# Seven block products in place of eight for two of eight pairs of inner tiles, in ten gate and up groups of a feed-forward stage

## The chip, the cores and the metric

The kernel runs on one core of a Trainium2 chip. The metric is the device time of one execution in microseconds; lower is better. The core has five engines that run side by side and meet at semaphores: TensorE (PE in the profile, with PEld for its weight loads) does matmuls, VectorE (DVE) and ScalarE (ACT) do elementwise work, GpSimd (POOL) and SyncE (SP) issue transfers here. Each engine takes its instructions in the order in which the program lists them for it.

## The reference, cut to what matters

One encoder block: four parallel mixers, cross attention, and a gated feed-forward part, each added to the residual, and a last norm. The change lies in the feed-forward part, for 256 rows, `D_MODEL` 2048 and `D_FF` 5632, all in float32:

```python
def swiglu(h, w_gate_up, w_down):
    gate, up = jnp.split(h @ w_gate_up, 2, axis=-1)
    return (jax.nn.silu(gate) * up) @ w_down

x = x + swiglu(rms_norm(x, norm_g[l, 2]), w_gate_up[l], w_down[l])
```

## The kernel before

**Float32 products in three matmuls.** The weights and activations are float32. Each operand is kept as a high part, rounded to the matmul's operand type, and a low part, the difference. A product of a 128x128 block of activations and a 128x512 block of weights is three matmuls into one PSUM bank: high by high, high by low, low by high (`part_rows`, L349, L350, L351). The activations are the stationary operand, the weights the moving one. An activation tile has 512 columns: 256 rows high, 256 rows low.

**The weight stream.** All weights arrive in one stream of slabs of 16 blocks of 128x128, that is 128x2048, 1 MB each, in the order in which they are used (`Stream`, L61 to L121). SP loads a slab into one of three `raw` buffers (L81). `_half` (L75) prepares half a slab, a piece of 1024 columns, at a time: ScalarE copies it to the high part `wh` (L102), VectorE subtracts to get the low part `wl` (L103). `take` (L107) hands out four blocks at a time; at the start of each piece it lets `_half` run so far ahead that two further pieces are prepared or in preparation, three if an extra pool `st.extra` is open. There are three pairs of `wh` and `wl` buffers, and a fourth with the extra pool, so the copy of a piece waits until TensorE is done with the piece that had its buffer.

**The background.** Work that isn't on the main path is written as generators. `Background.poll` (L160), called after each product, steps a generator if its due time has come and if VectorE owes little by the program's own accounts; `drain` (L165) steps one to its end at once. The program order that results is fixed when the kernel is built.

**The gate and up stage** (`gate_up`, L874) has 11 groups of 512 columns of the gate and the same 512 of the up half. A group goes through 16 inner tiles of 128 for the gate (16 x 2 row halves = 32 products, into two banks), then the same for up; together 64 products and 8 slabs. `gate` (L879) takes SiLU from the gate's banks on ScalarE (L882). `up` (L884) multiplies on VectorE (L206), transposes (L390) and stores to the tensor `hidden` in HBM through POOL. The first group takes the inner tiles in parts, since the last of them arrive late; groups 1 to 10 are alike (L928 to L930). The background task `fetch` (L891) loads tiles of `hidden` back (L397) and splits them into the feature tiles `f` (L210, L202): 28 of 44 beside the groups (L927), the last 16 in the next stage (L932), since they lie in `self.h3`, the activation tiles that the groups still read.

**The down stage** (`down`, L934) goes through the 44 feature tiles four times, two products a step, and forces `fetch` on if a feature tile isn't ready three steps ahead.

Of the kernel before, what the change touches and what calls it, by code (L numbers as in the profile page):

```python
# [34 lines left out]
CUTS = {0: [0, 256, 512, 1024, 2048]}  # L35
# [25 lines left out]
class Stream:  # L61


    def __init__(self, tc, pools, W, bg):
        self.tc, self.nc, self.W, self.bg = tc, tc.nc, W, bg
        self.rawp, self.wp = pools
        self.order = []
        self.n = 0
        self.after = []
        self.halves = []  # L70
        self.raw = None
        self.extra = None
        self.places = []

    def _half(self):  # L75

        nc, n = self.nc, 8 * len(self.halves)
        if n % 16 == 0:
            self.raw = self.rawp.tile([P, 2048], F32, name="raw", tag="raw")
            for a, b in zip(CUTS[n], CUTS[n][1:]) if n in CUTS else [(0, 1024), (1024, 2048)] if self.after else [(0, 2048)]:  # L80
                (nc.scalar if (n, a) == (0, 0) else nc.sync).dma_start(self.raw[:, a:b], self.W[n // 16][:, a:b])  # L81
                if self.after:
                    self.after.pop(0)()
# [12 lines left out]
        pool = self.extra if self.extra and len(self.halves) % 4 == 3 else self.wp  # L96
        wh, wl = (pool.tile([P, 1088], F32R, name=t, tag=t) for t in ("wh", "wl"))
        at = 48 if any(a <= n < b for a, b in ROWS) else 8
        wh, wl = wh[:, at:at + 1024], wl[:, at:at + 1024]
        edges = [0, 256, 512, 1024] if n == 0 else [0, 512, 1024] if n == 8 else [0, 1024]  # L100
        for a, b in zip(edges, edges[1:]):
            nc.scalar.copy(wh[:, a:b], r[:, a:b])  # L102
            nc.vector.tensor_tensor(out=wl[:, a:b], in0=r[:, a:b], in1=wh[:, a:b].bitcast(F32), op=ALU.subtract)  # L103
        self.bg.dve(1024)
        self.halves.append((wh, wl))

    def take(self, w, k, c, nb=1):  # L107
        if self.n % 8 == 0:
            ahead = self.n // 8 + 1 + min(3 if self.extra else 2, self.n // 16)
            while len(self.halves) < min(ahead, NBLK // 8):  # L110
                self._half()
        half, o = self.halves[self.n // 8], (self.n % 8) * P
        if self.n >= NBLK - HELD:
            (wh, wl), o = half[o // 512], 0
        else:
            wh, wl = half
        self.order += [(w, k, c + i * P) for i in range(nb)]
        self.n += nb
        if self.n % 8 == 0:
            self.halves[self.n // 8 - 1] = None  # L120
        return wh[:, o:o + nb * P], wl[:, o:o + nb * P]  # L121


class Background:
# [17 lines left out]
    def first(self, g):  # L142

        self.q.sort(key=lambda e: e[0] is not g)
# [29 lines left out]
class Block:  # L174
# [25 lines left out]
    def tt(self, out, a, b, op):  # L200
        self.bg.dve(math.prod(out.shape[1:]))
        self.nc.vector.tensor_tensor(out=out, in0=a, in1=b, op=op)  # L202
# [139 lines left out]
    def part_rows(self, p, r, slot, wh, wl, start, stop, narrow=False):  # L342

        if narrow:
            for c in (slice(0, R), slice(R, 512)):
                self.part_rows(p[:, c], r, slot, wh[:, c], wl[:, c], start and c.start == 0, stop)
            return
        hi, lo = slot[:, r * P:(r + 1) * P], slot[:, R + r * P:R + (r + 1) * P]
        self.nc.tensor.matmul(p, hi, wh, start=start, stop=False)  # L349
        self.nc.tensor.matmul(p, hi, wl, start=False, stop=False)  # L350
        self.nc.tensor.matmul(p, lo, wh, start=False, stop=stop)  # L351
        self.bg.pe(0.68 * wh.shape[1] / 512)

    def gemm_rows(self, w, cols, slots, done=None, parts=None, before=None, out=None):

# [506 lines left out]
    def mlp(self):  # L862
        tc, nc, act = self.tc, self.nc, self.act
        with tc.tile_pool(name="fp", bufs=1) as fp:
            self.gap(fp, 192)
            f = act[4:12] + [fp.tile([P, 512], F32R, name=f"f{i}") for i in range(20)] + self.h3
            with tc.tile_pool(name="gp", bufs=2) as gp:
                self.gate_up(gp, f)
# [5 lines left out]
    def gate_up(self, gp, f):  # L874

        nc = self.nc
        box, g, stored = {}, {}, []

        def gate(ps):  # L879
            for r in range(2):  # L880
                g[r] = gp.tile([P, 512], F32, name=f"g{r}", tag=f"g{r}")
                nc.scalar.activation(g[r], ps[r], AF.Silu, scale=box["col"][:, r:r + 1])  # L882

        def up(j, ps):  # L884
            for r in range(2):
                h, u = (gp.tile([P, 512], F32, name=n, tag=n) for n in ("h", "u"))
                self.stt(h, ps[r], box["col"][:, r:r + 1], g[r], ALU.mult, ALU.mult)
                self.store_turned(self.ff, 4 * j, r, u, h)
            stored.append(self.bg.now)

        def fetch(k0, k1, ahead, pause, wait=0):  # L891
# [32 lines left out]
        self.bg.drain(col)  # L924
        gate(ps[0])
# [722 lines left out]
```

## Time and profile before

| | |
|---|---|
| time, three runs | 1462.64, 1463.66 and 1462.53 us, median 1462.64 |
| profiled execution | span 1461.5 us from first to last instruction; its own time is not listed apart from the runs |
| granted TensorE clock | mean 0.998 |
| moved by DMA | 320.15 MB, mean 219 GB/s |
| loads of `raw` by SP | 246 of 1024 KB, 11 of 512 KB |

How to read it: all times are microseconds unless marked ns. Part 1 of the page has busy time and share of each engine, part 2 cuts the span into 40 slices with busy tenths, part 4 follows the chain of work that ended last back from the end, part 5 lists groups of instructions with line, engine, operation, output, inputs and count, then busy time, the mean of one in ns, and the engine's idle time just before them with what ended it. In the order of single instructions the columns are start, duration, engine, line, operation, output, inputs and count, and in brackets the idle time before. Neighbouring instructions of one engine can overlap, so a duration can be longer than the distance between two starts.

### The profile page before, as it was taken

Reading aid. Unit: us, or ns where it says so; the run is one execution under the profiler, and the core shown is the slowest. Engines: PE = TensorE matmul, PEld = TensorE weight load, DVE = VectorE, ACT = ScalarE, POOL = GpSimd, SP = SyncE. Lnnn points to the kernel's source line nnn. Section 1 sums busy time; section 2 is a strip of 40 time slices with the busy share of each in tenths; the row PEclk is TensorE's granted clock in tenths of the full one; section 3 lists DMA queues with packets and bytes.
Section 4 is the critical chain, followed back from the end, with each engine's and each line's share of the span. In section 5 each row is a group of like instructions: output and inputs, shape, how many; then the busy total and the mean of one; then the engine's idle time right before and its main releaser. Section 6 shows DMA issues by size and latency. Waiting matters only on the chain.

```text
span 1461.5 us, 17996 instructions
## 1 busy us (share of the span) xinstructions
PE 1452.1 (99%) x6724; PEld 1206.9 (83%) x6724; DVE 920.9 (63%) x1319; ACT 735.2 (50%) x1048; POOL 207.8 (14%) x276
## 2 busy tenths in 40 slices
PE   9999999999999999999999999999999999999997
PEld 7888888888888888888888888888888888888886
DVE  6668868777887676676665555455555456444445
ACT  7566655447555465565554444444444445434344
POOL 0000100012302333530411110011110011000000
PEclk9999999999999999999999999999999999999999
DMA  9877555456757788864867666666766666555554
GB/s 353 295 284 248 200 200 173 145 202 211 229 185 243 243 251 260 253 209 150 257 227 228 213 218 211 213 215 228 229 206 212 216 217 219 198 193 186 197 201 144
DMA packets 60071, 320.15 MB, mean 219 GB/s; under 512 B 9517, under 2 KB 11214, under 8 KB 28368
## 3 DMA queue, kind: packets, MB, share of 16 engines
q1 hardware_dynamic: 46208, 281.11, 56.0%
q0 software_dynamic: 13344, 37.24, 9.8%
q8 instruction: 52, 0.85, 0.2%
q10 hardware_dynamic: 432, 0.66, 0.1%
q14 instruction: 35, 0.29, 0.1%
HBM read 298.52 MB, written 20.45 MB: 218 GB/s over the span
## 4 chain that ended last, share of the span: by engine, by line
PE 99%; DMA 0%; ACT 0%; SPq 0%; DVE 0%; issue 0%
PE pg L349 29%; PE pg L351 29%; PE pg L350 29%; PE pg L300 4%; PE pg L301 2%; PE pm L1101 1%; PE pm L855 1%; PE pm L351 1%; PE pm L349 1%; PE pm L350 1%; PE pm L826 1%; DMA raw<-in_W 0%; PE pm L1510 0%; PE pm L827 0%; PE pm L1275 0%; PE pm L1062 0%
## 5 line engine op out<-in xcount | busy, mean ns | idle before, releaser
L103 DVE TENSOR_TENSOR wl<-raw,wh 128x1024 fp32r<-128x1024 f32 (+1 forms) x503 | 611.5, 1216 | 477.5 <-ACT wh L102 476.5
L102 ACT CAST wh<-raw 128x1024 fp32r<-128x1024 f32 (+1 forms) x503 | 524.0, 1043 | 597.8 <-PE pg L351 527.5
L349 PE MATMUL pg<-wh,act 128*128 128x512 f32 (+1 forms) x1666 | 650.2, 390 | 0.1
L350 PE MATMUL pg<-wl,act 128*128 128x512 f32 (+1 forms) x1666 | 648.4, 389 | 0.5 <-DVE wl L103 0.5
L351 PE MATMUL pg<-wh,act 128*128 128x512 f32 (+1 forms) x1666 | 648.6, 389 | 0.0
L349 PEld LDWEIGHTS pg<-wh,act 128*128 128x128 f32 x1666 | 313.0, 188 | 66.4 <-issue 1.5
L351 PEld LDWEIGHTS pg<-wh,act 128*128 128x128 f32 x1666 | 312.9, 188 | 65.6 <-DVE act L202 0.2
L350 PEld LDWEIGHTS pg<-wl,act 128*128 128x128 f32 x1666 | 313.0, 188 | 65.1 <-DVE wl L103 1.1
L300 PE MATMUL pg<-act,wh 128*128 128x512 f32 x256 | 90.5, 395 | 0.0
L301 PE MATMUL pg<-act,wl 128*128 128x256 f32 x256 | 71.8, 280 | 0.0
L392 POOL DMA_DIRECT2D hidden<-u x22 | 16.7, 763 | 386.5 <-DVE u L390 386.5
L300 PEld LDWEIGHTS pg<-act,wh 128*128 128x128 f32 x256 | 48.1, 188 | 10.5
L351 PE MATMUL pg<-wh,f 128*128 128x512 f32 x140 | 54.5, 389 | 0.0
L349 PE MATMUL pg<-wh,f 128*128 128x512 f32 x140 | 54.5, 389 | 0.0
L350 PE MATMUL pg<-wl,f 128*128 128x512 f32 x140 | 54.5, 389 | 0.0
L301 PEld LDWEIGHTS pg<-act,wl 128*128 128x128 f32 x256 | 48.2, 188 | 0.2
L397 POOL DMA_DIRECT2D tmp<-hidden x44 | 38.9, 890 | 39.5 <-ACT wh L102 24.3
L392 POOL DMA_DIRECT2D features<-tmp x32 | 22.8, 717 | 95.9 <-DVE tmp L390 95.9
L351 PEld LDWEIGHTS pg<-wh,f 128*128 128x128 f32 x140 | 26.3, 188 | 5.5
L350 PEld LDWEIGHTS pg<-wl,f 128*128 128x128 f32 x140 | 26.3, 188 | 5.4
L349 PEld LDWEIGHTS pg<-wh,f 128*128 128x128 f32 x140 | 26.3, 188 | 5.3
L397 POOL DMA_DIRECT2D ar<-features x24 | 21.1, 888 | 20.7 <-DMA features<-tmp 13.0
(314 smaller groups left out, 1046.0 us busy)
## 6 DMA issues: line engine op xcount, KB each, us to landing
raw<-in_W SPq DMA_DIRECT2D x246, 1024.0 KB, 5.0
raw<-in_W SPq DMA_DIRECT2D x11, 512.0 KB, 7.0
hidden<-u POOLq DMA_DIRECT2D x22, 256.0 KB, 3.5
tmp<-hidden POOLq DMA_DIRECT2D x44, 128.0 KB, 5.1
features<-tmp POOLq DMA_DIRECT2D x32, 128.0 KB, 2.7
ar<-features POOLq DMA_DIRECT2D x24, 128.0 KB, 6.5
k<-in_mem SPq DMA_DIRECT2D x8, 256.0 KB, 7.6
keys<-k POOLq DMA_DIRECT2D x8, 256.0 KB, 7.4
```

The source lines that it names most:

```text
L102: nc.scalar.copy(wh[:, a:b], r[:, a:b])
L103: nc.vector.tensor_tensor(out=wl[:, a:b], in0=r[:, a:b], in1=wh[:, a:b].bitcast(F32), op=ALU.subtract)
L300: self.nc.tensor.matmul(p[:, :], wh, slot[:, :], start=start, stop=False)
L301: self.nc.tensor.matmul(p[:, 0:R], wl, slot[:, 0:R], start=False, stop=stop)
L349: self.nc.tensor.matmul(p, hi, wh, start=start, stop=False)
L350: self.nc.tensor.matmul(p, hi, wl, start=False, stop=False)
L351: self.nc.tensor.matmul(p, lo, wh, start=False, stop=stop)
L392: self.nc.gpsimd.dma_start(to[r], u.rearrange("p (k c) -> p k c", c=P))
L397: self.nc.gpsimd.dma_start(t.rearrange("p (g t) -> p g t", t=32), src)
L826: nc.tensor.matmul(p[:, :], q[d][:, r * P:(r + 1) * P], kt[d][:, :], start=d == 0, stop=False)
L855: nc.tensor.matmul(p[:, 0:R], v[m][:, s], pt[m][:, c:c + R], start=m == 0 and v is vh and c == 0, stop=m == 1 and v is vl)
L1101: self.b.nc.tensor.matmul(p, a, b, start=start and n == 0, stop=stop and n == 2)
```

## The change

In groups 1 to 10, the inner tiles 0 and 1, and 2 and 3, are taken as two pairs. For a pair, the activations are a 2x2 block matrix (two row halves by two inner tiles), and the weights are one too (two inner tiles by gate and up). Their block product is done in seven products in place of eight. The other twelve tiles are taken as before.

The plan of a group is `GROUP = "NNSNNSNN"`, one letter per slab. N is a slab as before. S is the slab of a pair: `_sums` makes four pieces of it, of 1024, 512, 1024 and 1024 columns; ahead of the third it sums blocks of `raw` in place, four additions of 512 columns on VectorE. The pieces serve 2, 1, 2 and 2 products, each against one 128x128 block of activations. Three of a pair's seven use activations as they are, four use combinations that `combine` makes in new tiles `z`, once, between group 0 and group 1.

```diff
+GATE_UP = 1920 // 16 + 8
+GROUP = "NNSNNSNN"
+
+PAIRED = {GATE_UP + 8 * j + i for j in range(10) for i, x in enumerate(GROUP) if x == "S"}
...
+    def _sums(self):
+
+        nc, r, ph = self.nc, self.raw, self.phase
+        o, m = ((0, 1024), (1024, 512), (0, 1024), (1024, 1024))[ph]
+        wh, wl = self._buffers(self.made, m)
+        if ph == 2:
+            s = [r[:, i * 512:i * 512 + 512] for i in range(4)]
+            for out, a, b in ((1, 1, 3), (3, 0, 3), (0, 0, 1), (2, 0, 2)):
+                nc.vector.tensor_tensor(out=s[out], in0=s[a], in1=s[b], op=ALU.add)
+            self.bg.dve(2048, 4)
+        src = r[:, o:o + m]
+        nc.scalar.copy(wh, src)
+        nc.vector.tensor_tensor(out=wl, in0=src, in1=wh.bitcast(F32), op=ALU.subtract)
+        self.bg.dve(src.shape[1])
+        self.halves.append((wh, wl))
+        self.phase = (ph + 1) % 4
+        if ph == 3:
+            self.made += 16
+
+    def _fill(self):
+
+        ahead = self.at + 1 + min(3 if self.extra else 2, self.n // 16)
+        while len(self.halves) < ahead and self.made < NBLK:
+            self._half()
...
+    def combine(self, z, a, b):
+
+        tt, t, u, v, w = self.tt, *(self.tmp() for _ in range(4))
+        for x, y in ((t, a), (u, b)):
+            tt(x, y[:, 0:R].bitcast(F32), y[:, R:512].bitcast(F32), ALU.add)
+        yield SOON
+        tt(v[:, 0:P], t[:, P:R], u[:, P:R], ALU.subtract)
+        tt(w[:, 0:P], t[:, 0:P], t[:, P:R], ALU.subtract)
+        tt(v[:, P:R], v[:, 0:P], t[:, 0:P], ALU.subtract)
+        tt(w[:, P:R], u[:, 0:P], v[:, P:R], ALU.add)
+        yield SOON
+        for i, x in enumerate((v, w)):
+            self.split2(z[:, i * R:i * R + R], z[:, 512 + i * R:512 + i * R + R], x)
```

`paired_rows` takes gate and up together. Its products go to eight PSUM banks: four of the pool `pg` for gate and up by row half (`a0`, `a1`, `b0`, `b1`), and four of the pool `pm` for the products 1, 5, 6 and 7, which several results share. Both S slabs add into the same banks. The shared ones are combined behind the second S (`mixed`), then the gate is finished (`gated`); up is finished at the group's end (`upped`).

```diff
+        for kind in plan:
+            if kind == "S":
...
+                pairs = iter((("1", a[0]), ("b0", x4), ("a0", a[1]), ("6", s2), ("7", s3), ("a1", a[2]), ("5", x1)))
+                for parts in st.take_sums(w, ks, cols):
+                    for wh, wl in parts:
+                        name, (hi, lo) = next(pairs)
+                        put(name, hi, lo, wh, wl)
+                        self.bg.poll()
+                done += 1
+                if done == s:
+                    mixed(*(q[i] for i in "1567"))
...
+            if first and done == s and n >= len(rest):
+                first(q["a0"], q["a1"])
+                first = None
...
+        def mixed(q1, q5, q6, q7):
+
+            g[0], g[1], h[0], h[1] = (gp.tile([P, 512], F32, name=n, tag=n) for n in ("g0", "g1", "h", "h"))
+            nc.scalar.copy(g[0], q1)
+            self.tt(h[0], g[0], q6, ALU.add)
+            self.tt(g[1], h[0], q7, ALU.add)
+            self.tt(h[0], q5, h[0], ALU.subtract)
+            self.tt(h[1], q5, g[1], ALU.subtract)
+
+        def gated(*ps):
+
+            for r in range(2):
+                self.tt(g[r], g[r], ps[r], ALU.add)
+                nc.scalar.activation(g[r], g[r], AF.Silu, scale=box["col"][:, r:r + 1])
+
+        def upped(j, ps):
+
+            for r in range(2):
+                self.tt(h[r], h[r], ps[r], ALU.add)
+            up(j, h, h)
```

The rest in the stage: the extra pool (`wy`, a fourth pair of weight buffers) is open throughout it, the combinations are drained between groups 0 and 1, and `z` is used again for four feature tiles, so that 24 feature tiles are fetched beside the groups and 20 in the down stage.

```diff
+            with tc.tile_pool(name="wy", bufs=1) as self.st.extra, tc.tile_pool(name="gp", bufs=2) as gp:
+                self.gate_up(gp, f, z)
+                self.st.extra = None
...
+        sums = [((2 * i, 2 * i + 1), z[i]) for i in range(GROUP.count("S"))]
+        comb = self.bg.add(combined())
         gate(ps[0])
         up(0, ps[1])
-        early = self.bg.add(fetch(0, FT - 16, 3, 2.0, 15))
+        early = self.bg.add(fetch(0, FT - 20, 3, 2.0, 15))
+        self.bg.drain(comb)
         for j in range(1, DFF // 512):
-            gate(self.gemm_rows("w_gate_up", [j * 512], self.h3)[0])
-            up(j, self.gemm_rows("w_gate_up", [DFF + j * 512], self.h3)[0])
+            upped(j, self.paired_rows("w_gate_up", [j * 512, DFF + j * 512], self.h3, sums, GROUP, mixed, gated))
         self.bg.drain(early)
-        self.bg.add(fetch(FT - 16, FT, 6, SOON))
+        self.bg.add(fetch(FT - 20, FT, 6, SOON))
```

More of the change, by code (lines that the diff above doesn't have):

```diff
@@ L67, in __init__ @@
         self.order = []
-        self.n = 0
+        self.n = self.made = 0
         self.after = []
         self.halves = []
+        self.at = self.phase = 0
         self.raw = None
@@ L73, in __init__, with _buffers, _load @@
         self.places = []
-    def _half(self):
[L77 to L83, printed above, removed]
+    def _buffers(self, n, m):
+        pool = self.extra if self.extra and len(self.halves) % 4 == 3 else self.wp
+        at = 48 if any(a <= n < b for a, b in ROWS) else 8
+        return (pool.tile([P, 1088], F32R, name=t, tag=t)[:, at:at + m] for t in ("wh", "wl"))
+    def _load(self, n):
+        nc = self.nc
+        self.raw = self.rawp.tile([P, 2048], F32, name="raw", tag="raw")
+        for a, b in zip(CUTS[n], CUTS[n][1:]) if n in CUTS else [(0, 1024), (1024, 2048)] if self.after else [(0, 2048)]:
+            (nc.scalar if (n, a) == (0, 0) else nc.sync).dma_start(self.raw[:, a:b], self.W[n // 16][:, a:b])
+            if self.after:
+                self.after.pop(0)()
+    def _half(self):
+        nc, n = self.nc, self.made
+        if n % 16 == 0 and self.phase == 0:
+            self._load(n)
+        if n // 16 in PAIRED:
+            return self._sums()
+        self.made += 8
         o = (n % 16) * P
@@ L95, in _half @@
             return
[L96 to L99, printed above, removed]
+        wh, wl = self._buffers(n, 1024)
         edges = [0, 256, 512, 1024] if n == 0 else [0, 512, 1024] if n == 8 else [0, 1024]
@@ L105, in _half, with _used @@
         self.halves.append((wh, wl))
-    def take(self, w, k, c, nb=1):
[L108 to L112, printed above, removed]
+    def _sums(self):
[19 more added lines that the diff above has]
+            self._half()
+    def _used(self):
+        self.halves[self.at] = None
+        self.at += 1
+    def take(self, w, k, c, nb=1):
+        o = (self.n % 8) * P
+        if o == 0:
+            self._fill()
+        half = self.halves[self.at]
         if self.n >= NBLK - HELD:
@@ L119, in take, with take_sums @@
         if self.n % 8 == 0:
-            self.halves[self.n // 8 - 1] = None
+            self._used()
         return wh[:, o:o + nb * P], wl[:, o:o + nb * P]
+    def take_sums(self, w, ks, cols):
+        assert self.n // 16 in PAIRED and self.n % 16 == 0
+        self.order += [(w, ks[k], cols[c] + i * P) for k, c in ((0, 0), (1, 1), (1, 0), (0, 1)) for i in range(4)]
+        for ph in range(4):
+            self._fill()
+            wh, wl = self.halves[self.at]
+            yield [(wh[:, a:a + 512], wl[:, a:a + 512]) for a in range(0, wh.shape[1], 512)]
+            self._used()
+        self.n += 16
 class Background:
@@ L347, in part_rows, with part @@
             return
-        hi, lo = slot[:, r * P:(r + 1) * P], slot[:, R + r * P:R + (r + 1) * P]
+        self.part(p, slot[:, r * P:(r + 1) * P], slot[:, R + r * P:R + (r + 1) * P], wh, wl, start, stop)
+    def part(self, p, hi, lo, wh, wl, start, stop):
         self.nc.tensor.matmul(p, hi, wh, start=start, stop=False)
@@ new lines, in paired_rows, with put @@
+    def paired_rows(self, w, cols, slots, sums, plan, mixed, first, hold=None, ready=None):
+        st, s, nk = self.st, len(sums), len(slots)
+        rest = [k for k in range(nk) if not any(k in ks for ks, _ in sums)]
+        steps = [(c, k) for c in range(2) for k in rest]
+        todo, q = iter(sums), {}
+        count = {"a0": len(rest) + s, "a1": len(rest) + s, "b0": len(rest) + s, "b1": len(rest)}
+        left, total = {}, 0
+        def put(name, hi, lo, wh, wl):
+            if name not in q:
+                q[name] = self.gbank() if name in count else self.bank()
+                left[name] = count.get(name, s)
+            new = left[name] == count.get(name, s)
+            left[name] -= 1
+            self.part(q[name][:, :], hi, lo, wh, wl, new, left[name] == 0)
+        form = lambda t, r: (t[:, r * P:(r + 1) * P], t[:, R + r * P:R + (r + 1) * P])
+        n = done = 0
+        for kind in plan:
+            if kind == "S":
+                ks, z = next(todo)
+                a = [form(slots[ks[0]], 0), form(slots[ks[1]], 0), form(slots[ks[1]], 1)]
+                x1, s2, s3, x4 = ((z[:, i * P:i * P + P], z[:, 512 + i * P:512 + i * P + P]) for i in range(4))
+                pairs = iter((("1", a[0]), ("b0", x4), ("a0", a[1]), ("6", s2), ("7", s3), ("a1", a[2]), ("5", x1)))
[7 more added lines that the diff above has]
+                    mixed(*(q[i] for i in "1567"))
+            else:
+                for c, k in steps[n:n + 4]:
+                    if ready:
+                        ready(k)
+                    wh, wl = st.take(w, k, cols[c], 4)
+                    for r in range(2):
+                        put("ab"[c] + str(r), *form(slots[k], r), wh, wl)
+                        self.bg.poll()
+                n += 4
+            if first and done == s and n >= len(rest):
+                first(q["a0"], q["a1"])
+                first = None
+        assert n == len(steps) and done == s
+        return q["b0"], q["b1"]
@@ L865, in mlp @@
             self.gap(fp, 192)
-            f = act[4:12] + [fp.tile([P, 512], F32R, name=f"f{i}") for i in range(20)] + self.h3
-            with tc.tile_pool(name="gp", bufs=2) as gp:
-                self.gate_up(gp, f)
+            f = [fp.tile([P, 512], F32R, name=f"f{i}") for i in range(16)]
+            z = [fp.tile([P, 1024], F32R, name=f"z{i}") for i in range(2)]
+            f = act[4:12] + f + [z[i // 2][:, i % 2 * 512:i % 2 * 512 + 512] for i in range(4)] + self.h3
+            with tc.tile_pool(name="wy", bufs=1) as self.st.extra, tc.tile_pool(name="gp", bufs=2) as gp:
+                self.gate_up(gp, f, z)
+                self.st.extra = None
             with tc.tile_pool(name="hp", bufs=1) as hp:
@@ L882, in gate, with up @@
                 nc.scalar.activation(g[r], ps[r], AF.Silu, scale=box["col"][:, r:r + 1])
-        def up(j, ps):
+        def up(j, ps, h=None):
+            h = h or [gp.tile([P, 512], F32, name="h", tag="h") for _ in range(2)]
             for r in range(2):
-                h, u = (gp.tile([P, 512], F32, name=n, tag=n) for n in ("h", "u"))
-                self.stt(h, ps[r], box["col"][:, r:r + 1], g[r], ALU.mult, ALU.mult)
-                self.store_turned(self.ff, 4 * j, r, u, h)
+                u = gp.tile([P, 512], F32, name="u", tag="u")
+                self.stt(h[r], ps[r], box["col"][:, r:r + 1], g[r], ALU.mult, ALU.mult)
+                self.store_turned(self.ff, 4 * j, r, u, h[r])
             stored.append(self.bg.now)
+        def mixed(q1, q5, q6, q7):
[10 more added lines that the diff above has]
+        def upped(j, ps):
+            for r in range(2):
+                self.tt(h[r], h[r], ps[r], ALU.add)
+            up(j, h, h)
+        h = {}
         def fetch(k0, k1, ahead, pause, wait=0):
@@ L924, in gate_up, with combined @@
         self.bg.drain(col)
+        def combined():
+            for ks, z in sums:
+                yield from self.combine(z, *(self.h3[k] for k in ks))
+                yield
+        sums = [((2 * i, 2 * i + 1), z[i]) for i in range(GROUP.count("S"))]
+        comb = self.bg.add(combined())
         gate(ps[0])
         up(0, ps[1])
-        early = self.bg.add(fetch(0, FT - 16, 3, 2.0, 15))
+        early = self.bg.add(fetch(0, FT - 20, 3, 2.0, 15))
+        self.bg.drain(comb)
         for j in range(1, DFF // 512):
-            gate(self.gemm_rows("w_gate_up", [j * 512], self.h3)[0])
-            up(j, self.gemm_rows("w_gate_up", [DFF + j * 512], self.h3)[0])
+            upped(j, self.paired_rows("w_gate_up", [j * 512, DFF + j * 512], self.h3, sums, GROUP, mixed, gated))
         self.bg.drain(early)
-        self.bg.add(fetch(FT - 16, FT, 6, SOON))
+        self.bg.add(fetch(FT - 20, FT, 6, SOON))
     def down(self, f):
```

2 lines of the change are left out of this document (1 added, 1 removed).

## The prediction

> **What bounds the kernel now.** I read first the page's shares and slices, then the chain of waits, then the costliest groups and the waits, then the order of single instructions in the gate and up stage (about 735 to 1214 us).
>
> ```profile
> span 1461.5 us, 17996 instructions
> PE 1452.1 (99%) x6724; PEld 1206.9 (83%) x6724; DVE 920.9 (63%) x1319; ACT 735.2 (50%) x1048; POOL 207.8 (14%) x276
> PEclk9999999999999999999999999999999999999999
> PE 99%; DMA 0%; ACT 0%; SPq 0%; DVE 0%; issue 0%
> L350 PE MATMUL pg<-wl,act 128*128 128x512 f32 (+1 forms) x1666 | 648.4, 389 | 0.5 <-DVE wl L103 0.5
> L103 DVE TENSOR_TENSOR wl<-raw,wh 128x1024 fp32r<-128x1024 f32 (+1 forms) x503 | 611.5, 1216 | 477.5 <-ACT wh L102 476.5
> L102 ACT CAST wh<-raw 128x1024 fp32r<-128x1024 f32 (+1 forms) x503 | 524.0, 1043 | 597.8 <-PE pg L351 527.5
> ```
>
> TensorE is the path: 99% of the chain, at the full clock, with 0.5 us of idle time ahead of 1666 matmuls. ScalarE waits for TensorE (a weight buffer must come free), and VectorE waits for ScalarE. So any matmul taken out shortens the kernel, as long as the two preparing engines keep up.
>
> A matmul's mean of 389 ns is not its price, because neighbours overlap. The price is the distance of starts:
>
> ```profile
> 899.66 0.39 PE L350 MATMUL pg<-wl,act 128*128 128x512 f32 x1
> ...
> 900.34 0.39 PE L350 MATMUL pg<-wl,act 128*128 128x512 f32 x1
> ...
> 900.79 0.39 PE L349 MATMUL pg<-wh,act 128*128 128x512 f32 x1
> 778.10 1.40 DVE L206 SCALAR_TENSOR_TENSOR h<-pg,rc,g 128x512 f32<-128x512 f32 x2
> 779.42 1.29 DVE L390 STREAM_TRANSPOSE u<-h 128x512 f32<-128x512 f32 x2
> 780.63 1.19 DVE L103 TENSOR_TENSOR wl<-raw,wh 128x1024 fp32r<-128x1024 f32 x1
> 821.62 1.40 DVE L206 SCALAR_TENSOR_TENSOR h<-pg,rc,g 128x512 f32<-128x512 f32 x2
> ```
>
> One product (three matmuls, L349 to L351) takes 900.34 − 899.66 = 0.68 us. A group of 64 products takes 821.62 − 778.10 = 43.52 us, which is 64 × 0.68: no gaps.
>
> **The part removed.** Ten groups, two S rounds each, one product less per round: 20 products, 60 matmuls, 20 × 0.68 = **13.6 us** off TensorE (a group falls to 62 × 0.68 = 42.2). It lies wholly on the path.
>
> **The work added on the preparing engines.** Their prices, as starts or hand-overs:
>
> ```profile
> 900.99 1.05 ACT L102 CAST wh<-raw 128x1024 fp32r<-128x1024 f32 x1 [1.67 <-PE pg L351]
> 902.07 1.23 DVE L103 TENSOR_TENSOR wl<-raw,wh 128x1024 fp32r<-128x1024 f32 x1 [1.49 <-ACT wh L102]
> 912.95 1.23 DVE L103 TENSOR_TENSOR wl<-raw,wh 128x1024 fp32r<-128x1024 f32 x1 [0.58 <-ACT wh L102]
> 914.10 0.42 DVE L202 TENSOR_TENSOR f<-tmp,f 128x256 fp32r<-128x256 f32 x1
> 142.90 0.68 DVE L202 TENSOR_TENSOR k<-k,pm 128x512 f32<-128x512 f32 x1
> 143.50 1.67 DVE L206 SCALAR_TENSOR_TENSOR res<-res,vec,krs 128x256 f32<-128x256 f32 x4
> 392.99 0.42 DVE L202 TENSOR_TENSOR tmp<-tmp 128x256 f32<-128x256 f32 x1
> 393.32 0.75 DVE L202 TENSOR_TENSOR tmp<-pg,tmp 128x256 f32<-128x256 f32 x2
> 1448.90 0.16 DVE L956 SCALAR_TENSOR_TENSOR rc<-rc 128x1 f32<-128x1 f32 x1
> 1449.10 0.16 DVE L957 SCALAR_TENSOR_TENSOR rc<-rc 128x1 f32<-128x1 f32 x1
> 799.67 1.37 ACT L882 ACTIVATE g<-pg,rc 128x512 f32<-128x512 f32 x2 [0.99 <-PE pg L351]
> 800.94 1.04 ACT L102 CAST wh<-raw 128x1024 fp32r<-128x1024 f32 x1
> L210 ACT CAST f<-tmp 128x256 fp32r<-128x256 f32 x20 | 8.1, 403 | 0.0
> L218 ACT CAST w3h<-k 128x512 fp32r<-128x512 f32 x18 | 11.1, 625 | 7.2 <-DVE k L202 4.3 <-PE pm L1101 2.3 <-DMA k<-in_c 0.3
> L1115 ACT COPY k<-pm 128x512 f32<-128x512 f32 x8 | 4.7, 588 | 8.5 <-PE pm L1101 8.5
> L202 DVE TENSOR_TENSOR w3l<-pm,w3h 128x128 fp32r<-128x128 f32 x8 | 2.3, 283 | 0.0
> ```
>
> VectorE, independent neighbours: 1.15 for 1024 columns, 0.60 for 512, 0.33 for 256; a dependent neighbour waits for the end and 0.04 more (1448.90 to 1449.10 at 0.16), so 0.72 for 512. A copy starts 0.20 after TensorE's piece boundary (900.99 against 900.79), a subtraction 1.08 after its copy's start.
>
> An S round prepares 3584 columns for 7 products, where the slab had 2048 for 8, and adds four sums: VectorE 3 × 1.15 + 0.60 + 4 × 0.60 (one dependent, 0.12) = 6.6 us against TensorE's 4.76; ScalarE 3 × 1.05 + 0.62 = 3.8. A round alone does not fit under its own products; its neighbours must carry it. Over a whole group they can: VectorE 12 × 1.15 + 2 × 6.6 + eight 512-wide sums of the results (4.9) + up's four instructions (780.63 − 778.10 = 2.5) + 2.4 feature splits (0.8) = 35.2 of 42.2 us (83%); ScalarE 12 × 1.05 + 7.6 + 0.6 + 1.4 + 1.0 = 23. That such a load can stay hidden is shown here:
>
> ```profile
> core 0: us, PE busy (x) PEld busy (x) DVE busy (x) ACT busy (x) POOL busy (x), PEclk, DMA share, GB/s
> 125.00:150.00 25.00, 25.00 (x112) 20.60 (x111) 24.55 (x49) 17.01 (x28) 2.33 (x5) 1.00 0.60 201
> 865.00:908.00 43.00, 43.00 (x191) 35.65 (x190) 22.85 (x25) 19.25 (x22) 5.05 (x6) 1.00 0.67 220
> ```
>
> With VectorE at 98% (and the fourth weight buffer, as the change has it again) TensorE lost nothing.
>
> **Margins in the steady groups.** Let T be the start of the piece ahead of an S round; the round's four pieces are needed at T + 2.72, 4.08, 4.76 and 6.12 (the difference 0.23 later, at the second matmul). The four sums need no free buffer, so VectorE can start them at once behind the second piece's difference, at about T − 1.2 and, behind up's work, T − 0.6. The third ends at T + 1.3, copy to 2.4, difference to 3.7, needed 4.99: margin **1.3**. The fourth piece waits for the buffer freed at T + 2.72: copy 2.92 to 3.97, difference to 5.2, needed 6.35: margin **1.1**, and the same for the piece after. Behind the second S (end at X): difference of an earlier piece to X + 1.3, six result sums to 5.0, of which the first gate sum is whole at 4.5; two SiLUs to 5.8; only then ScalarE's copy of the group's last piece, to 6.9; difference to 8.2; needed X + 3 × 2.72 + 0.23 = 8.4: margin **0.2**, the smallest. All positive, so the steady stall is 0 by these rows; bounds 0 to 0.8 a group (margins missed by up to 0.5 in two places). As 0.2 is little I take 0.1 a group, **1.0 us**.
>
> **The passage into the first S group.** All of the combining of activations is drained at once between up(0) and group 1. TensorE's boundary is E = 776.95 − 1.28 + 2.72 = 778.39 (the last subtraction ahead of up starts at 776.95, 1.28 after a boundary); up ends at 780.63, E + 2.2.
>
> ```profile
> 776.95 1.23 DVE L103 TENSOR_TENSOR wl<-raw,wh 128x1024 fp32r<-128x1024 f32 x1 [1.50 <-ACT wh L102]
> ```
>
> A pair: two 256-wide sums 0.75, the 128-wide chain about 0.75 (283 ns is the nearest 128-wide row), copy 0.44, two differences 0.66: 2.6; both pairs 5.2, to E + 7.5 on VectorE. ScalarE is held until E + 7.2 by the pair's copies, so group 1's fourth piece is copied to 8.3 and its difference ends at 9.5, needed at 8.39: 1.1 late. The first S round then starts with no lead: differences to 11.2, three sums to 13.1, copy 14.2, difference 15.4, needed at about 14.3: 1.1 late again. Together **2.3 us**, once; bounds 0 (all of it overlaps up) and 5 (nothing does).
>
> **What costs nothing.** The weights' bytes and order of loads stay: 1 MB per slab. Slots come free later in an S round:
>
> ```profile
> SPq L81 <- DVE wl L103: 276.5, 55, 5.0
> DMA to landing us min/median/max: 4.7/5.0/7.2
> ```
>
> The load behind the first S waits on SP for the slot freed at T + 5.2 and lands at 10.5, when its first buffer comes free (10.4): covered at the median. At 7.2 us the second S's sums start 2.3 later and its third piece is about 0.5 late: bound 5 us over ten groups, inside the range. Four feature splits move into the down stage (4 × 0.33 VectorE), under products at 1.36 us per step; without that cover 1.3 us. The POOL loads move with them, issued six ahead.
>
> **Sum.** 1461.5 − 13.6 + 2.3 + 1.0 = 1451.2 us of span; the median of the runs, 1462.64, lies 1.1 above the profiled span, so **1452.3 us**, own range 1450 to 1456.
>
> **Rivals.** *All hidden*, the passage too: 1462.6 − 13.6 = 1449.0. For it: the 98% slice; against it: the drain in one lump.
>
> *VectorE instructions cost their listed durations* (1.23, 0.68) and not the spacings, 0.08 more each. At the group's last piece nine instructions in a row make 0.7, against 0.2 of margin: 0.5 a group, 5 in all; the passage (22 instructions) 4.1: 1462.6 − 13.6 + 9.1 = 1458.1. Against it: 142.90 to 143.50 is shorter than 0.68. For it: many additions depend on one another. [...]
>
> *The same, and copies wait for all four sums*: third pieces lose another 0.6 + 0.6 of their 1.3, some 0.3 each after give and take, 20 × 0.3 = 6: 1464.1, no change that can be told.
>
> *VectorE becomes the bound in the S rounds* (the slower side): where no lead is carried in, TensorE waits the whole 6.6 − 4.76 = 1.8 a round, 20 × 1.8 = 36: 1462.6 − 13.6 + 2.3 + 36 = 1487. It decides from 11.3 / 20 = 0.57 us a round. For it: 6.6 against 4.76, and in-order queues where one late wait holds everything behind. Against it: 83% over the group, and margins of 1.1 and more.
>
> [...]
>
> **How the numbers follow.** Forecast 0.50; all hidden 0.07; listed durations 0.22; with the wait for all sums 0.06; VectorE bound 0.15. Faster by over 0.2% (2.9 us, about what a measurement of this kernel tells from no change): 0.79; within it 0.06; slower 0.15. The range 1449 to 1461 holds the first three, 0.79.
>
> **What would show it.** TensorE has 6664 matmuls. The groups from the third on take 42.2 to 42.4 us between their first up instructions; group 1 takes about 44.5. TensorE idles, released by VectorE's differences, at the fourth piece of group 1 and at its first S, about 1.1 us each. I am wrong if a steady group takes over 43 us, if TensorE waits at third pieces in every S round, or if a matmul's spacing leaves 0.227 us.

## The result and the profile after

The changed kernel takes 1454.63 us (median of four runs, 1453.49 to 1454.97) against 1463.09 for the kernel before (four runs, 1462.53 to 1463.66): a ratio of 0.9942 with the interval [0.9928, 0.9956]. The forecast was 1452.3 with 1449 to 1461 as its range. The profiled execution of after took 1453.49, with a span of 1451.7.

The page of after, the lines that answer to those of before:

```profile
span 1451.7 us, 18199 instructions
PE 1442.7 (99%) x6664; PEld 1195.4 (82%) x6664; DVE 1053.5 (73%) x1535; ACT 773.2 (53%) x1102; POOL 207.1 (14%) x276
...
PEclk9999999999999999999999999999999999999999
...
PE 99%; DMA 0%; ACT 0%; SPq 0%; DVE 0%; issue 0%
...
L409 PE MATMUL pg<-wh,act 128*128 128x512 f32 (+1 forms) x1546 | 604.6, 391 | 0.0
L410 PE MATMUL pg<-wl,act 128*128 128x512 f32 (+1 forms) x1546 | 603.3, 390 | 0.2 <-DVE wl L120 0.2
```

The 60 matmuls are gone (6724 to 6664), VectorE has 216 instructions more, and TensorE is still 99% of the chain. By the idle times ahead of the matmuls it lost nothing: 0.0 and 0.2 us.

So the stage should be 13.6 us shorter. TensorE's order of instructions shows the first matmul of the stage and the first of the down stage (the one that reads `f`), in before:

```profile
745.75 0.39 PE L349 MATMUL pg<-wh,act 128*128 128x512 f32 x1
...
1224.47 0.39 PE L349 MATMUL pg<-wh,f 128*128 128x512 f32 x1
```

and in after, with a stretch of one group between:

```profile
745.07 0.39 PE L409 MATMUL pg<-wh,act 128*128 128x512 f32 x1
...
870.66 0.39 PE L409 MATMUL pg<-wh,act 128*128 128x512 f32 x1
...
871.34 0.39 PE L409 MATMUL pg<-wh,act 128*128 128x512 f32 x1
...
872.04 0.39 PE L409 MATMUL pg<-wh,act 128*128 128x512 f32 x1
...
872.74 0.39 PE L409 MATMUL pg<-wh,act 128*128 128x512 f32 x1
...
1214.70 0.39 PE L409 MATMUL pg<-wh,f 128*128 128x512 f32 x1
```

The stage went from 478.72 us, which is 704 products at 0.680, to 469.63, where 684 products at 0.680 would be 465.12. **4.5 us of the 13.6 came back inside the stage**, and the lower rows show how: a product takes 0.68 us up to 871.34 and 0.70 behind it. Over the stage, 683 of 2052 matmuls start 0.230 to 0.237 after their forerunner, the others 0.225 to 0.229, and none more than 0.24. Nothing waits; a third of the matmuls is a little slower. Their durations do not show it (0.39 in both kinds), nor does the busy share or the granted clock. (The stage also began 0.68 earlier in after, a difference that stands almost whole at the start of the program; the down stage takes 228.83 in both.)

VectorE's order of instructions in after: the combinations, the first instruction of up in groups 0 and 1, the shared sums of group 1, and the first instruction of up in groups 2 and 3:

```profile
737.91 0.42 DVE L259 TENSOR_TENSOR tmp<-act 128x256 f32<-128x256 f32 x1
...
751.03 0.76 DVE L259 TENSOR_TENSOR z<-tmp,z 128x256 fp32r<-128x256 f32 x2
...
777.63 1.40 DVE L263 SCALAR_TENSOR_TENSOR h<-pg,rc,g 128x512 f32<-128x512 f32 x2
...
812.68 0.68 DVE L259 TENSOR_TENSOR g<-h,pm 128x512 f32<-128x512 f32 x1
813.28 0.68 DVE L259 TENSOR_TENSOR g<-g,pg 128x512 f32<-128x512 f32 x1
...
821.44 1.41 DVE L263 SCALAR_TENSOR_TENSOR h<-h,rc,g 128x512 f32<-128x512 f32 x2
...
864.02 1.41 DVE L263 SCALAR_TENSOR_TENSOR h<-h,rc,g 128x512 f32<-128x512 f32 x2
...
906.60 1.41 DVE L263 SCALAR_TENSOR_TENSOR h<-h,rc,g 128x512 f32<-128x512 f32 x2
```

The combinations, listed in the program behind up of group 0 (777.63), ran from 737.91 to 751.8: from 7 us ahead of the stage's first matmul (745.07) until 7 us into group 0. A steady group takes 42.58 (906.60 − 864.02), not 42.16.

### The profile page after: what moved, and what is told of

Its sections match the earlier page's. It is cut to its first block, busy times and chain, and to the rows that moved or that the text cites. A ratio compares the mean times of both kernels' runs of the same rounds, so it can differ in the third digit from the quotient of the medians.

```text
span 1451.7 us, 18199 instructions
## 1 busy us (share of the span) xinstructions
PE 1442.7 (99%) x6664; PEld 1195.4 (82%) x6664; DVE 1053.5 (73%) x1535; ACT 773.2 (53%) x1102; POOL 207.1 (14%) x276
## 4 chain that ended last, share of the span: by engine, by line
PE 99%; DMA 0%; ACT 0%; SPq 0%; DVE 0%; issue 0%
PE pg L409 27%; PE pg L410 27%; PE pg L411 27%; PE pg L357 4%; PE pg L358 2%; PE pm L410 2%; PE pm L409 2%; PE pm L411 2%; PE pm L1260 1%; PE pm L981 1%; PE pm L952 1%; PE pm L1669 0%; DMA raw<-in_W 0%; PE pm L953 0%; PE pm L1434 0%; PE pm L1221 0%
## 5 line engine op out<-in xcount | busy, mean ns | idle before, releaser
L120 DVE TENSOR_TENSOR wl<-raw,wh 128x1024 fp32r<-128x1024 f32 (+1 forms) x463 | 557.3, 1214 | 279.0 <-ACT wh L119 278.1
L119 ACT CAST wh<-raw 128x1024 fp32r<-128x1024 f32 (+1 forms) x463 | 479.7, 1043 | 411.4 <-PE pg L411 333.6
L409 PE MATMUL pg<-wh,act 128*128 128x512 f32 (+1 forms) x1546 | 604.6, 391 | 0.0
L410 PE MATMUL pg<-wl,act 128*128 128x512 f32 (+1 forms) x1546 | 603.3, 390 | 0.2 <-DVE wl L120 0.2
L411 PE MATMUL pg<-wh,act 128*128 128x512 f32 (+1 forms) x1546 | 602.8, 390 | 0.0
L409 PEld LDWEIGHTS pg<-wh,act 128*128 128x128 f32 x1546 | 290.4, 188 | 62.6 <-issue 1.5
L411 PEld LDWEIGHTS pg<-wh,act 128*128 128x128 f32 x1546 | 290.3, 188 | 62.1 <-DVE act L259 0.2
L410 PEld LDWEIGHTS pg<-wl,act 128*128 128x128 f32 x1546 | 290.4, 188 | 61.4 <-DVE wl L120 1.1
L135 ACT CAST wh<-raw 128x1024 fp32r<-128x1024 f32 x80 | 75.3, 942 | 137.5 <-PE pg L411 102.9
L136 DVE TENSOR_TENSOR wl<-raw,wh 128x1024 fp32r<-128x1024 f32 x80 | 87.1, 1089 | 52.9 <-ACT wh L135 52.9
L132 DVE TENSOR_TENSOR raw<-raw 128x512 f32<-128x512 f32 x80 | 55.2, 690 | 1.9
L409 PE MATMUL pg<-wh,f 128*128 128x512 f32 x112 | 43.6, 390 | 0.0
L411 PE MATMUL pg<-wh,f 128*128 128x512 f32 x112 | 43.6, 390 | 0.0
L410 PE MATMUL pm<-wl,z 128*128 128x512 f32 x64 | 25.0, 391 | 0.0
```

The source lines that it names most:

```text
L132: nc.vector.tensor_tensor(out=s[out], in0=s[a], in1=s[b], op=ALU.add)
L135: nc.scalar.copy(wh, src)
L136: nc.vector.tensor_tensor(out=wl, in0=src, in1=wh.bitcast(F32), op=ALU.subtract)
```

## The experiments

**The first suspicion.** The slow products come in blocks of two or four, one piece in four: those of the fourth weight buffer. In after, all 516 matmuls that read a piece of this buffer start their successor 0.232 us or more behind them; of the other 167 slow ones, 163 lie among the five matmuls right behind such a piece. The program's allocation puts the fourth pair of buffers at bytes 192384 and 196736 of a partition, 128 past a multiple of 256; the three usual pairs (125120, 129472 and on) lie 192 past one. A piece starts 48 elements, 192 bytes, into its buffer (`at = 48` in `_buffers`). So usual pieces start 128 past a multiple of 256, those of the fourth buffer 64 past one. The activation tiles, stationary operands, start 128 past one. Below, a place is such a remainder: "moving 64, stationary 128".

**start128**: moves the pieces in the fourth buffer by 64 bytes and nothing else.

```diff
-        at = 48 if any(a <= n < b for a, b in ROWS) else 8
+        at = 64 if pool is self.extra and n >= 1920 else 48 if any(a <= n < b for a, b in ROWS) else 8
```

> The fourth weight buffer of the gate and up stage lies where it was, but its pieces start 64 bytes later in it, so that the moving operand starts at 128 bytes modulo 256 as in the three others (before: 64). Theory A (the start of the moving operand within its 256 bytes sets the pace of a matmul): every product of the stage takes 0.680 us, a group 42.16 in place of 42.58, the time falls by 4.6 us, from 1454.6 to about 1450.0. Rival B (the place of the fourth buffer, or the work of the other engines at that moment, slows TensorE): one piece in four stays at 0.700 a product, time 1454.6. Rival C (the missing 4.6 us are stalls of TensorE behind VectorE in the S rounds): no change, 1454.6.

Measured: 1449.85 us (1449.02 to 1450.91, four runs) against 1463.37, ratio 0.9904 [0.9887, 0.992]. TensorE's order, with the ends of the stage:

```profile
746.42 0.39 PE L409 MATMUL pg<-wh,act 128*128 128x512 f32 x1
...
870.86 0.39 PE L409 MATMUL pg<-wh,act 128*128 128x512 f32 x1
...
871.54 0.39 PE L409 MATMUL pg<-wh,act 128*128 128x512 f32 x1
...
872.22 0.39 PE L409 MATMUL pg<-wh,act 128*128 128x512 f32 x1
...
1211.54 0.39 PE L409 MATMUL pg<-wh,f 128*128 128x512 f32 x1
```

Every product takes 0.68, and the stage 465.12: the whole 13.60 is there. The place of the start, not the fourth buffer as such, cost 4.5 us. By TensorE's starts in after, 3.4 of it lie in the misplaced pieces themselves and 1.1 right behind them.

**all64**: the opposite. The usual pieces of this stage start at 64 too.

```diff
-        at = 48 if any(a <= n < b for a, b in ROWS) else 8
+        at = 32 if pool is not self.extra and 1920 <= n < 3328 else 48 if any(a <= n < b for a, b in ROWS) else 8
```

> The other way round: the pieces in the three usual weight buffers start at 64 bytes modulo 256 throughout the gate and up stage, the fourth stays at 64. Theory A: all products at about 0.700, a group 62 x 0.70 = 43.4, the stage 0.02 x 684 = 13.7 us longer than without any slow product, 9.1 longer than the changed kernel: about 1463.7. Rival B and rival C: groups stay at 42.58, 1454.6.

Measured: 1463.28 us (one run), the time of before. VectorE's order, the first instruction of up in groups 2 and 3:

```profile
867.23 0.75 DVE L263 SCALAR_TENSOR_TENSOR h<-h,rc,g 128x512 f32<-128x512 f32 x1
...
910.63 0.75 DVE L263 SCALAR_TENSOR_TENSOR h<-h,rc,g 128x512 f32<-128x512 f32 x1
```

A group takes 43.40 us and the stage 478.50, with 2007 of 2052 matmuls slow. With every piece at 64, the whole gain of the change is gone.

**start0** and **start192**: as start128, with 32 and 16 in place of 64 there, so that pieces in the fourth buffer start at 0 and at 192.

> The fourth buffer's pieces start at 0 modulo 256. Theory A with a grid of 128 bytes: fast as at 128, groups 42.16, 1450.0. Theory A with a grid of 256 bytes and its fast place at 128: groups 42.58 or more, 1454.6 or more. Rivals B and C: 42.58.

> The fourth buffer's pieces start at 192 modulo 256. Theory A with a grid of 128 bytes: slow as at 64, groups 42.58, 1454.6. Theory A with a grid of 64 bytes is already ruled out if 128 is fast. Rivals B and C: 42.58.

Measured: 1454.61 and 1454.22 us (one run each), groups of 42.51 and 42.60, stages of 469.31 and 469.85. Of the four places, 64, 0 and 192 cost about the same (4.2 to 4.7 us), and only 128 costs nothing. Either 128 is a good place for a moving operand, or what counts is that the stationary operand starts there too. The next two tell these apart.

**shiftact**: on start128, all activation tiles moved by 128 bytes (the gap behind them is shorter by as much): moving 128, stationary 0.

```diff
+        self.gap(cp, 128);
         self.act = [cp.tile([P, 512], F32R, name=f"act{i}") for i in range(24)]
...
-        self.gap(cp, 416)
+        self.gap(cp, 288)
```

> As start128, but all activation tiles act0 to act23 (stationary operands) begin 128 bytes later, at 0 modulo 256; the weights' buffers, z and the other feature tiles stay at 128. Theory A1 (the moving operand's own start counts): gate and up stage unchanged, products 0.680, groups 42.16, 1449.9. Theory A2 (moving and stationary operands must begin at the same place of their 256 bytes): products against act tiles go to about 0.70, those against z stay at 0.680: groups 42.16 + 54 x 0.02 = 43.2, stage some 12 us longer, and the down stage slower in the same way.

VectorE's order in shiftact, the first instruction of up in groups 2 and 3:

```profile
878.56 1.41 DVE L263 SCALAR_TENSOR_TENSOR h<-h,rc,g 128x512 f32<-128x512 f32 x2
...
921.77 1.41 DVE L263 SCALAR_TENSOR_TENSOR h<-h,rc,g 128x512 f32<-128x512 f32 x2
```

**both0**: on shiftact, the weights moved along: moving 0, stationary 0. The combinations `z` stay at 128.

```diff
-        at = 64 if pool is self.extra and n >= 1920 else 48 if any(a <= n < b for a, b in ROWS) else 8
+        at = 32 if pool is self.extra and n >= 1920 else 16 if any(a <= n < b for a, b in ROWS) else 8
```

> As shiftact, but the weights' pieces are moved by 128 bytes too, so that activation tiles and pieces both start at 0 modulo 256; z and the feature tiles of their own pool stay at 128. Theory A2 (same place within 256 bytes): products against act tiles back at 0.680, group 0 at 43.52 as in start128 (44.61 in shiftact); only those against z (8 of 62) and their neighbours slow, groups 42.3 to 42.5; the down stage slow against 20 of its 44 feature tiles, some 3 us; about 1455. Theory A1 (the moving operand must start at 128): group 0 at 44.6 or more, groups 43.4, about 1476.

Measured: shiftact 1476.30 us (one run) with groups of 43.2 and a stage of 476.61; both0 1454.94 (one run) with group 0 back at 43.52, steady groups of 42.41 and a stage of 467.66. So 128 for the moving operand is not enough (shiftact), and 0 and 0 is as fast as 128 and 128 (group 0 of both0). Even within both0 the two kinds stand side by side. TensorE's order there, the start of a product with `z` and of the next:

```profile
875.86 0.39 PE L409 MATMUL pm<-wh,z 128*128 128x512 f32 x1
...
876.55 0.39 PE L409 MATMUL pm<-wh,z 128*128 128x512 f32 x1
```

It takes 0.69. Over the group the eight products with `z` (moving 0, stationary 128) take 0.702 us on the mean and the 54 with `act` (0 and 0) 0.681. Eight times 0.022 is 0.17 of the 0.25 us by which the group is longer than start128's 42.16. The rest falls to neighbours: the matmuls with `act` right ahead of a product with `z` start it 0.232 to 0.235 behind them. As a whole both0 is 5 us slower than start128. Its stage begins 1.0 earlier and is 2.5 longer, and its down stage is 3.1 longer, as was expected of the feature tiles that stay at 128. Of shiftact's 26 us over start128, 11.5 lie in the stage, 11.4 ahead of it (its first matmul starts at 757.83 in place of 746.42) and 3.1 in the down stage. Tiles moved there as well, but these parts were not taken apart.

**before4**: the kernel before, with the fourth buffer open in this stage, at 64 as in the changed kernel.

```diff
-            with tc.tile_pool(name="gp", bufs=2) as gp:
+            with tc.tile_pool(name="wy", bufs=1) as self.st.extra, tc.tile_pool(name="gp", bufs=2) as gp:
                 self.gate_up(gp, f)
+                self.st.extra = None
```

> The kernel before with nothing but the fourth weight buffer in the gate and up stage, its pieces at 64 modulo 256. Theory A: one piece in four of 64 products slow, 0.4 us a group as in group 0 of the changed kernel (43.92), 11 x 0.4 = 4.4 us slower than before, 1467.5 or so, with VectorE as idle as before. Rival (a fourth buffer costs nothing as long as VectorE isn't loaded): 1463.

Measured: 1467.22 us (one run) against 1462.88, groups of 43.92 in place of 43.52 and a stage of 483.04, 648 of its 2112 matmuls slow. VectorE's order, the first instruction of up in groups 2 and 3:

```profile
865.72 1.40 DVE L206 SCALAR_TENSOR_TENSOR h<-pg,rc,g 128x512 f32<-128x512 f32 x2
...
909.64 1.40 DVE L206 SCALAR_TENSOR_TENSOR h<-pg,rc,g 128x512 f32<-128x512 f32 x2
```

The 4.3 us come without any block product. That they belong to the buffer's place, and not to the buffer, is shown by start128 in the changed kernel; before4 was not run with the buffer at 128.

**three**: the changed kernel without the fourth buffer.

```diff
-            with tc.tile_pool(name="wy", bufs=1) as self.st.extra, tc.tile_pool(name="gp", bufs=2) as gp:
+            with tc.tile_pool(name="gp", bufs=2) as gp:
                 self.gate_up(gp, f, z)
-                self.st.extra = None
```

> The changed kernel without the fourth weight buffer (three in the gate and up stage, as before the change; so no piece starts at 64 modulo 256 either). Theory M (the prediction's margins are real and the fourth buffer makes them): a piece less of lead, some 1 us of TensorE lost in each S round and 2.3 at the piece behind the mixed results, groups near 46.5, about 1450 + 43 = 1493. Rival N (VectorE and ScalarE have room enough with three): groups at 42.16, 1450.

Measured: 1456.44 us (one run), groups of 42.74 to 42.97 and a stage of 472.25. TensorE's order around the third pieces of the two S slabs of one group:

```profile
876.74 0.61 PE L409 MATMUL pm<-wh,z 128*128 128x512 f32 x2
877.30 0.50 PE L410 MATMUL pm<-wl,z 128*128 128x512 f32 x1
...
877.64 0.40 PE L411 MATMUL pm<-wh,z 128*128 128x512 f32 x1
...
892.70 0.61 PE L409 MATMUL pm<-wh,z 128*128 128x512 f32 x2
893.40 0.50 PE L410 MATMUL pm<-wl,z 128*128 128x512 f32 x1
893.74 0.39 PE L411 MATMUL pm<-wh,z 128*128 128x512 f32 x1
```

TensorE takes the first matmuls of both products of the third piece (the L409 rows of two, which need no `wl`), and then waits for the difference. Three spacings of 0.227 would be 0.68; from the pair to the L411 row it takes 0.90 and 1.04, so 0.22 and 0.36 are lost. With some 0.2 in spacings of up to 0.27 right behind, that is the 0.8 by which the group is longer than start128's 42.16. The fourth buffer is worth 472.25 − 465.12 = 7.1 us here. That it is a gain was expected, but at six times the size.

**inplace**: on start128, the combinations are held at their place in the program.

```diff
-        self.bg.drain(comb)
+        mark = self.mark(); self.bg.drain(comb); self.keep_place(mark)
```

> As start128 (all four buffers at 128 modulo 256), but the combinations of activations are held where the program lists them, between up(0) and group 1; in the changed kernel they had run 25 to 40 us earlier, beside group 0. Theory P (the prediction's price of the passage was right and only its place was wrong): TensorE stalls 2.3 us at group 1 and its first S round, 1449.9 + 2.3 = 1452.2, group 1 takes 44.5 in place of 42.16. Rival Q (VectorE would have hidden the passage wherever it lay): group 1 at 42.16, 1449.9.

Measured: 1449.55 us (1449.32 to 1449.78, four runs) against 1462.88, ratio 0.9908 [0.9892, 0.9925]; not to be told from start128. VectorE's order from up of group 0 on, and up of group 1:

```profile
777.35 1.40 DVE L263 SCALAR_TENSOR_TENSOR h<-pg,rc,g 128x512 f32<-128x512 f32 x2
...
779.89 0.72 DVE L259 TENSOR_TENSOR tmp<-act 128x256 f32<-128x256 f32 x2
780.52 1.22 DVE L120 TENSOR_TENSOR wl<-raw,wh 128x1024 fp32r<-128x1024 f32 x1
781.66 0.69 DVE L259 TENSOR_TENSOR tmp<-tmp 128x128 f32<-128x128 f32 x3
...
788.56 0.43 DVE L259 TENSOR_TENSOR z<-tmp,z 128x256 fp32r<-128x256 f32 x1
...
821.25 1.41 DVE L263 SCALAR_TENSOR_TENSOR h<-h,rc,g 128x512 f32<-128x512 f32 x2
```

Now the combinations run behind up, from 779.89 to 789.0, between the pieces' differences and not in one lump. From up to up group 1 takes 43.90, where start128 has 43.40 (822.16 − 778.76): the passage costs 0.5 us. TensorE's starts say the same, 42.66 against 42.16. (From up to up, group 1 is longer than it is on TensorE, since two result sums now stand ahead of up.)

**pairs3**: on start128, a third pair of inner tiles, to load VectorE on purpose. Ten more products fall away (6.8 us).

```diff
-GROUP = "NNSNNSNN"
+GROUP = "NSNNSNSN"
...
-            f = [fp.tile([P, 512], F32R, name=f"f{i}") for i in range(16)]
-            z = [fp.tile([P, 1024], F32R, name=f"z{i}") for i in range(2)]
-            f = act[4:12] + f + [z[i // 2][:, i % 2 * 512:i % 2 * 512 + 512] for i in range(4)] + self.h3
+            f = [fp.tile([P, 512], F32R, name=f"f{i}") for i in range(14)]
+            z = [fp.tile([P, 1024], F32R, name=f"z{i}") for i in range(3)]
+            f = act[4:12] + f + [z[i // 2][:, i % 2 * 512:i % 2 * 512 + 512] for i in range(6)] + self.h3
...
-        early = self.bg.add(fetch(0, FT - 20, 3, 2.0, 15))
+        early = self.bg.add(fetch(0, FT - 22, 3, 2.0, 15))
...
-        self.bg.add(fetch(FT - 20, FT, 6, SOON))
+        self.bg.add(fetch(FT - 22, FT, 6, SOON))
```

> As start128, with three pairs in each group (plan NSNNSNSN; three z tiles, 22 feature tiles fetched beside the groups). Ten products less: 6.8 us off TensorE if it keeps up, groups 61 x 0.68 = 41.48, 1443.1. VectorE's load by the prediction's prices is 39.5 of 41.5 us (95%). Theory M (VectorE's rounds stay covered as long as its sum over the group fits and pieces run ahead): groups at 41.5 to 42, time 1443 to 1448. Rival V (VectorE becomes the bound in the S rounds once the load passes some 90%): TensorE waits at third pieces, groups over 42.16, time over 1449.9.

Measured: 1489.40 us (1487.94 to 1493.21, four runs) against 1462.85, ratio 1.0182 [1.0164, 1.02]; groups take 44.1 to 48.05 us. Two rows of the waits (total, times, longest), and then TensorE's order at one of them, with the idle time in brackets:

```profile
ACT wh L135 <- DVE raw L132: 96.0, 26, 5.7
...
PE pm L409 <- ACT wh L135: 17.7, 9, 2.1
```

```profile
1053.17 0.39 PE L411 MATMUL pg<-wh,act 128*128 128x512 f32 x1
1055.68 0.73 PE L409 MATMUL pm<-wh,z 128*128 128x512 f32 x2 [2.12 <-ACT wh L135]
...
1057.92 0.59 PE L410 MATMUL pm<-wl,z 128*128 128x512 f32 x1
1058.30 0.63 PE L411 MATMUL pm<-wh,z 128*128 128x512 f32 x1
1058.73 0.63 PE L410 MATMUL pm<-wl,z 128*128 128x512 f32 x1
...
1061.29 0.43 PE L409 MATMUL pg<-wh,act 128*128 128x512 f32 x1
1061.56 0.39 PE L410 MATMUL pg<-wl,act 128*128 128x512 f32 x1
```

and the busy times in one stretch of 40 us and in 2 us of the passage above (order of columns: TensorE, its weight loads, VectorE, ScalarE, GpSimd, then the granted clock):

```profile
860.00:900.00 40.00, 37.45 (x156) 29.89 (x155) 34.06 (x42) 17.30 (x20) 4.16 (x5) 0.96 0.60 220
1058.00:1060.00 2.00, 2.00 (x6) 1.52 (x5) 1.46 (x2) 0.18 (x1) 0.00 (x0) 0.50 0.40 74
```

The rival of the slower side comes true with one pair more: TensorE waits some 2 us at a time for the copy of a third piece, which waits for its sums. VectorE is not full on the mean (34.06 of 40), though TensorE's waits stretch that mean; the waits lie at the third pieces, so what does not fit is the round and not the sum over the group. Seven of the nine waits are then paid again. In the one shown the matmuls start 0.43 apart, at about half rate, up to 1061.29, and the granted clock is 0.50. Behind the waits that end at 966.67 and 1011.28 us, of 2.12 and 1.84 like the others, the clock stays at 1.00.

## Why the prediction was right, and where it was not

The range held the time, but the forecast came within 2.3 us by two errors of opposite sign, and that is luck: 3.3 us of stalls did not come, and 4.5 us came from a term that had been put at nothing.

- **The part removed, 13.6 us: right to the digit.** start128 shows 478.72 − 465.12 = 13.60 where nothing else touches the stage.
- **The fourth weight buffer, costed at nothing: the step that failed.** The prediction took it as a cover and named VectorE's 98% slice, in which "TensorE lost nothing". That slice could not have shown the cost: its fourth buffer is of another pool (`wx`), which the program's allocation puts at 151232, 192 past a multiple of 256 like the usual ones. As a cover it is worth 7.1 us (three against start128). But its place makes the matmuls of one piece in four slower, 4.5 us in all: shown by start128, which moves the start alone; before4 agrees, where the buffer costs as much without the rest of the change. The prediction's own condition, that "a matmul's spacing leaves 0.227 us", is what happened.
- **The passage, 2.3 us forecast: 0.** The step took VectorE's order from the order in which the program lists its instructions. The built program does not always keep the order in which the kernel lists the instructions of an engine: the combinations, which need only the activations, ran 26 us and more before up of group 0, and stayed behind it where inplace held them. Had the place held, the lump was still the wrong picture: inplace shows them between the pieces, at 0.5 us.
- **Steady groups, 1.0 us forecast: 0.** No wait on TensorE in the stage can be seen in after, and start128's groups take 42.16, which is 62 × 0.68. VectorE's load was well sized: 35.2 of 42.2 forecast, and this row of after shows 36.26 of 42.58 over one group, by durations and not by distances of starts:

```profile
864.02:906.60 42.58, 42.58 (x187) 34.89 (x187) 36.26 (x45) 22.93 (x28) 5.03 (x6) 1.00 0.62 222
```

- **"All hidden", 1449.0, is what the mechanism does**: start128 and inplace at 1449.85 and 1449.55. The fourth buffer's place then took 4.5 us from it and the forecast added 3.3 of stalls that did not come.
- **Listed durations**: refuted. Two sums of group 1 that do not need each other, of 0.68 each, start at 812.68 and 813.28, 0.60 apart.
- **VectorE as the bound** is not this kernel but its neighbour: with two pairs the pieces run far enough ahead, with three (pairs3) they do not, and the sign of the change turns.
- **Loads and feature splits, nothing**: the down stage takes 228.83 in both kernels.

Open: why the starts matter (what the moving and the stationary read share is not seen in any row), what steps finer than 64 bytes would do, whether other equal pairs (64 and 64, 192 and 192) are fast too, and whether a matmul's own stationary tile or the one loaded beside it counts: neighbours of slow products are in part slow too, ahead of them in both0 and behind them in after.

The version that beats both kernels is start128 (or inplace, the same within the runs): 13 us faster than before.

## What to carry to other kernels

Price a matmul by the distance of starts, buffer by buffer, and not by its duration, the busy share or the idle time: these three were blind to 4.5 us here. When a change opens another buffer for a moving operand, look where it starts against the stationary one. And before a lump of work is priced at its place in the program, ask whether anything holds it there.

## What the runs showed of the hardware

- A matmul of this form (128x512, float32 operands) started 0.227 us after its forerunner where moving and stationary operand both started 128 past a multiple of 256 bytes (start128, 465.12 us for 2052) or both 0 past one (group 0 of both0, 43.52 us for 192), and later in the four other pairs of places tried: 0.233 on the mean for 64 against 128 (all64, 478.50 us for 2052) and 0.232 for 128 against 0 (group 0 of shiftact, 44.61 us for 192). The places 0 and 192 against 128, in one piece of four, cost 4.2 and 4.7 us of the stage (start0, start192). With all pieces of the stage at 64, it was 13.4 us of 465 (all64). All six pairs come from this stage; other forms were not tried.
- After a wait of 2.1 us TensorE ran at half rate for some 3.4 us (pairs3: starts 0.43 apart from 1057.92 to 1061.29, granted clock 0.50 from 1058 to 1060); over a stretch of 40 us the clock shows little of it (0.96 from 860 to 900). The same followed seven of nine waits of 1.8 to 2.1 us; behind the other two, of 2.12 and 1.84 us, the clock stayed at 1.00. So the length of the wait alone does not decide it, and what else does was not shown.
